# Seven up-projection channel tiles of a decoder layer computed by seven block products

## The chip, the cores and the metric

The kernel runs on one core of one Trainium2 chip. The metric is the device time of one execution in microseconds. Time before: 835.13 us, the median of 3 runs (834.89 to 835.53).

## The reference

One decoder layer for 512 tokens of width 1024, in float32. What matters here is its end, the channel mixer:

```python
u2 = _rmsnorm(h, norm2_g[l])
z = _causal_dwconv(u2 @ w_ffn_up[l], ffn_dw_w[l], ffn_dw_b[l])
h = h + (jax.nn.silu(z[..., :FFN_DIM]) * z[..., FFN_DIM:]) @ w_ffn_down[l]
return _rmsnorm(h, final_g)
```

FFN_DIM is 2816, so the up projection has 2 x 22 tiles of 128 channels: tile i is the gate (the half that goes through silu), tile 22 + i the value. The depthwise convolution is causal and three wide. Before this part stand the input projection, a convolution branch, a gated linear attention branch and the projection w_o, whose result is added to the residual.

## The kernel before

**Precision.** A float32 product is made of three: every operand is split into a high part (a cast to fp32r) and a low part (the rest), and `mm3` (L328) multiplies low by high, high by low and high by high into one PSUM bank. TensorE has the two parts of one operand as its stationary tile (128 x 128) and streams the other.

**Weights.** `order` (L162 to L178) lists every weight block in the order of use. `load` (L184) takes the next of the list into one of four `raw` buffers with a transfer issued by SyncE, four blocks ahead. `split_weight` (L254) makes the parts: ScalarE casts raw to `whi` (L281), VectorE subtracts to `wlo` (L290). For blocks in the set `ADDED` (L44) the low part is made otherwise: ScalarE writes the negated high part (L283), and a transfer in GpSimd's queue adds the same weights from DRAM (L284 is its issue). `whi` and `wlo` have four buffers each. `weight` (L299) hands a block out and splits up to `LOOK` = 2 further ones; it also calls `fill` (L312), which issues pieces of side work from `chains`, so many for each block.

**The up projection.** A channel tile is made by `col_tile` (L336): 8 k tiles (the 1024 inputs, 128 at a time) times three products, 24 products with the weights as stationary tile and all 512 tokens streaming. `GROUPS` (L34) lists 11 pairs of channel tiles, in three groups of 4, 3 and 4. For each pair (p, q) of a group: gate and value tile of p, `first_of_pair` (L1257), then gate and value tile of q, `second_of_pair` (L1265). Both call `glu` (L1243): per tile one ScalarE operation and two VectorE operations read the PSUM bank (`ffn_conv`, L1235), then a silu on ScalarE and a product on VectorE. They then form the sums and differences of halves of the two results that the down projection needs, and split them. The very first pair of group 0 is made in two halves of 256 tokens (L1358 to L1362), since the second half of the tokens is ready later.

**Seven block products.** The projections w_r, w_o and w_down are computed already by a scheme that cuts both operands in 2 x 2 blocks and needs seven block products instead of eight, with sums of blocks as operands. `seven` (L1128) runs it for w_o and, after each group, for w_down; its steps are named a11, a12, s1, n2, s4, n3 and a22, in the order of `STEPS` (L48). The sums of weight blocks are made by accumulating transfers in GpSimd's queue (`sum_on` L243, `add_n3` L232) and on VectorE (L240).

**PSUM.** Five banks have the tag `mm`, three `ax` (L124 to L128). A new tile of a tag waits until a bank of that tag is released by its readers.

**Between w_o and the up projection.** `o_complete` (L1212) makes the normed rows of a token tile as soon as its residual is complete. `to_channels` (L424) turns them with eight transposes into two `ax` banks, and `spread_gain` (L413) multiplies by the gain and splits: per bank four ScalarE operations of 128 x 128 for the high parts (L420) and four VectorE operations for the low parts (L422). Token tiles 0 and 1 are turned within w_o's last steps (`o_at`, L1219), tiles 2 and 3 between the first up tiles (L1361).

The order of the instructions on each engine is fixed when the program is built: they are queued by priority in the order written, and one that isn't ready lets later ones go ahead.

Of the kernel before, what the change touches and what calls it, by code (L numbers as in the profile page):

```python
# [17 lines left out]
P = 128  # L18
# [25 lines left out]
ADDED = {("w_glu", 2 * k) for k in range(1, KT)} | {(name, m) for name in ("w_gb", "w_gla") for m in range(KT)}  # L44
SEVEN = {"w_o": KT // 2, "w_down": FT // 2, "w_r": KT // 2}
# [27 lines left out]
def trunk_layer(ctx: ExitStack, tc: tile.TileContext, a: dict, out: bass.AP):  # L73
# [102 lines left out]
    for gi, pairs in enumerate(GROUPS):  # L176
        order += [("w_up", j) for pair in pairs for i in pair for j in (i, FT + i)]
        order += [("w_down", (pairs, step, d)) for step, d in STEPS]  # L178
# [5 lines left out]
    def load():  # L184
        if len(raws) < len(order):
            name, j = order[len(raws)]
            if name in SEVEN:
                raws.append(load_block(name, *j))
                return
            raw = raw_tile()  # L190
            nc.sync.dma_start(raw, a[name][j])
            raws.append(raw)
# [49 lines left out]

    def sum_on(name, pairs, step, d):  # L243

        where = {"a11": (0, 1), "n2": (1, 0)}
        if name == "w_r":
            where["s1"] = (1, 1)
            if (step, d) in (("n2", 1), ("s4", 0)):
                add_n3(name, pairs, 0 if step == "n2" else 1)
        if step in where:  # L250
            nxt = block(name, pairs, d, *where[step])
            nc.gpsimd.dma_start(kept[pairs, d], nxt, accum_op=ALU.add)  # L252

    def split_weight(between=None):  # L254
        if len(ready) < len(order):
# [4 lines left out]
            if name in SEVEN:  # L260
                raw = operand(name, raw, *spec)
                n = raw.shape[-1]
                hi = wp.tile([P, D], F32R, tag="whi", name=nm("whi"), bufs=4)[:, :n]
# [3 lines left out]
                sum_on(name, *spec)  # L267
# [145 lines left out]
    def spread_gain(banks, which, dst, groups=(0, 1)):  # L413
        for g in groups:
            c = which * KT + g * 4
            parts = [
                (*dst(g, k), banks[g][:, k * P : (k + 1) * P], gains[:, c + k : c + k + 1]) for k in range(4)
            ]
            for hi, _, tr, gain in parts:
                nc.scalar.activation(hi, tr, AF.Copy, scale=gain)  # L420
            for hi, lo, tr, gain in parts:
                nc.vector.scalar_tensor_tensor(lo, tr, gain, hi.bitcast(F32), ALU.mult, ALU.subtract)  # L422

    def to_channels(x, u, t, which):  # L424
        part = lambda g, k: tuple(u[g][i][:, k, t * P : (t + 1) * P] for i in range(2))
        spread_gain(turned(x), which, part)
# [792 lines left out]
    def o_at(step, i):  # L1219
        if (step, i) == ("n3", 1):  # L1220
            u2.extend(new_acts())
            to_channels(normed[0], u2, 0, 1)
        if (step, i) == ("a22", 0):
            to_channels(normed[1], u2, 1, 1)
# [8 lines left out]
    gain3 = load_gain("final_g")  # L1233
# [23 lines left out]
    def first_of_pair(i, accs):  # L1257

        w = fp.tile([P, 3 * H], F32, tag="w", name=nm("w"), bufs=2)
# [5 lines left out]
    def second_of_pair(i, accs, w, acts):  # L1265

        f = fp.tile([P, T], F32, tag="f", name=nm("f"), bufs=2)
        glu(i, accs, f)
        v = fp.tile([P, 3 * H], F32, tag="v", name=nm("v"), bufs=2)
# [80 lines left out]

    for gi, pairs in enumerate(GROUPS):
        acts = []
        early = {}
        if gi == 0:
# [3 lines left out]
            for lo in (0, T // 2):  # L1358
                for j, (w, acc) in enumerate(zip(ws, accs)):
                    col_tile(w, acts2, acc, lo, lo + T // 2)  # L1360
                    if lo == 0 and 1 <= j <= 2:  # L1361
                        to_channels(normed[j + 1], u2, j + 1, 1)  # L1362
            early = {pairs[0][0]: accs[:2], pairs[0][1]: accs[2:]}

# [3 lines left out]
        for p, q in pairs:  # L1368
            w, found = first_of_pair(p, both(p))
            acts.append(second_of_pair(q, both(q), w, found))  # L1370
        if gi < len(GROUPS) - 1:
# [93 lines left out]
```

## Time and profile before

| | |
|---|---|
| median of 3 runs | 835.13 us |
| profiled execution | 836.23 us |
| span of its instructions | 834.2 us |
| granted TensorE clock | 0.999 |
| feed-forward part (first up product to last full-width down product) | 479.3 to 824.5 us |
| VectorE busy in it | 253.99 us |
| ScalarE busy in it | 163.14 us |

Times in the profile are microseconds from the start of the span. PE is TensorE's matmul, PEld its weight load, DVE VectorE, ACT ScalarE, POOL GpSimd, SP SyncE; L281 is line 281 of the kernel. A group is written as line, engine, operation, out<-in, shapes, then x and the number of instructions, the busy time in us, the mean duration in ns, and the idle time of the engine before them with what ended it. A row of waits reads: engine, tile and line that waited, whom for, us in total, times, longest. A row of a timeline reads: start, duration, engine, line, operation, out<-in, shapes, number. A row of stages reads: stretch, its length, then for PE, PEld, DVE, ACT and POOL the busy time and the number of instructions, the granted clock, the share of the DMA engines and GB/s. A row of transfers gives the number, KB each and the median us from issue to landing.

### The profile page before, as it was taken

To read this page: it belongs to the slowest core of one execution; us is meant where nothing else is said; L and a number is where in the kernel's file an instruction comes from. 1 tells how busy PE (TensorE), PEld (TensorE's weight loads), DVE (VectorE), ACT (ScalarE), POOL (GpSimd) and SP (SyncE) were. 2 spreads that over 40 slices of the span, in tenths; PEclk is the share of its full clock that TensorE was granted. 3 is DMA by queue.
4 is the path that set the end of the run, shared out by engine and by line. 5 is a ranking of instruction groups with operands and counts; after the bars stand their busy time and mean duration, and the time that the engine had idled before them with its cause. 6 is when DMAs were issued, how large, how long until landed. Compare 5 with 4: busy or idle time off the path is not lost.

```text
span 834.2 us, 10185 instructions
## 1 busy us (share of the span) xinstructions
PE 823.8 (99%) x3817; PEld 686.7 (82%) x3817; DVE 645.3 (77%) x957; ACT 415.9 (50%) x606; POOL 69.6 (8%) x95
## 2 busy tenths in 40 slices
PE   9999999999999999999999999999999999999996
PEld 7888887888888888888888798888888888888885
DVE  5999966989899991865789658778757787667696
ACT  6853437762533553148534765444434444444454
POOL 1000102000111121000001000001000010000111
PEclk9999999999999999999999999999999999999999
DMA  9875547732546578321447544234842348222462
GB/s 341 273 214 140 137 125 158 221 101 86 128 113 157 131 199 197 102 84 57 138 100 188 169 150 140 89 97 104 214 152 88 66 87 286 98 88 97 101 126 102
DMA packets 41377, 117.72 MB, mean 141 GB/s; under 512 B 3984, under 2 KB 12448, under 8 KB 41328
## 3 DMA queue, kind: packets, MB, share of 16 engines
q1 hardware_dynamic: 33232, 88.82, 31.3%
q0 software_dynamic: 7920, 28.05, 20.0%
q8 instruction: 30, 0.49, 0.2%
q10 hardware_dynamic: 176, 0.20, 0.1%
q14 instruction: 19, 0.16, 0.1%
HBM read 114.96 MB, written 6.29 MB: 145 GB/s over the span
## 4 chain that ended last, share of the span: by engine, by line
PE 86%; DMA 4%; issue 4%; ACT 2%; DVE 2%; POOL 1%; SPq 0%; POOLq 0%; ACTq 0%; DVEq 0%
PE mm L332 26%; PE mm L333 26%; PE mm L334 26%; DMA kept<-in_w_o_dram 2%; PE mm L581 1%; PE ax L332 1%; PE ax L999 1%; PE ax L333 1%; PE ax L334 1%; DMA x<-in_x_dram 1%; DMA kept<-rows 1%; DMA raw<-in_w_o_dram 1%; PE ax L1001 1%; PE ax L981 1%; DMA hres<-in_x_dram 1%
## 5 line engine op out<-in xcount | busy, mean ns | idle before, releaser
L332 PE MATMUL mm<-uh,wlo 128*128 128x512 f32 (+1 forms) x704 | 269.8, 383 | 0.0
L334 PE MATMUL mm<-uh,whi 128*128 128x512 f32 (+1 forms) x704 | 267.3, 380 | 0.0
L333 PE MATMUL mm<-ul,whi 128*128 128x512 f32 (+1 forms) x704 | 267.1, 379 | 0.0
L688 DVE SCALAR_TENSOR_TENSOR c<-h,pp,c 128x507 f32<-128x507 f32 (+21 forms) x240 | 162.3, 732 | 1.2 <-ACT c L685 0.6
L333 PEld LDWEIGHTS mm<-ul,whi 128*128 128x128 f32 x704 | 132.5, 188 | 25.0 <-ACT h L1082 0.2
L332 PEld LDWEIGHTS mm<-uh,wlo 128*128 128x128 f32 x704 | 132.5, 188 | 24.9 <-issue 0.2
L334 PEld LDWEIGHTS mm<-uh,whi 128*128 128x128 f32 x704 | 132.4, 188 | 25.0
L281 ACT CAST whi<-raw 128x1024 fp32r<-128x1024 f32 x108 | 112.0, 1044 | 55.7 <-PE mm L334 45.6
L1240 DVE SCALAR_TENSOR_TENSOR tmp<-mm,pp,tmp 128x511 f32<-128x511 f32 x88 | 65.9, 748 | 66.7 <-ACT tmp L1238 65.5
L290 DVE TENSOR_TENSOR wlo<-raw,whi 128x1024 fp32r<-128x1024 f32 x85 | 103.2, 1220 | 14.7 <-ACT whi L281 14.4
L1238 ACT ACTIVATE tmp<-mm,pp 128x512 f32<-128x512 f32 x44 | 34.3, 779 | 60.8 <-PE mm L334 60.8
L283 ACT ACTIVATE wlo<-raw 128x1024 fp32r<-128x1024 f32 x23 | 24.4, 1061 | 74.0 <-PE mm L332 68.5
L266 DVE TENSOR_TENSOR wlo<-kept,whi 128x1024 fp32r<-128x1024 f32 (+1 forms) x40 | 46.4, 1167 | 15.4 <-ACT whi L265 15.2
L265 ACT CAST whi<-kept 128x1024 fp32r<-128x1024 f32 (+1 forms) x40 | 40.1, 1006 | 33.5 <-PE mm L334 14.3
L265 ACT CAST whi<-raw 128x1024 fp32r<-128x1024 f32 (+1 forms) x30 | 29.8, 1005 | 20.1 <-PE mm L334 18.8
L266 DVE TENSOR_TENSOR wlo<-raw,whi 128x1024 fp32r<-128x1024 f32 (+1 forms) x30 | 34.6, 1166 | 5.3 <-ACT whi L265 5.2
L1160 DVE TENSOR_TENSOR hres<-hres,mm 128x512 f32<-128x512 f32 (+1 forms) x49 | 32.6, 671 | 3.4 <-PE mm L334 2.8
L252 POOL DMA_DIRECT2D kept<-in_w_down_dram x12 | 10.3, 859 | 271.8 <-DVE wlo L266 271.8
L333 PE MATMUL mm<-wlo,sh 128*128 128x512 f32 x66 | 25.8, 391 | 0.0
L334 PE MATMUL mm<-whi,sh 128*128 128x512 f32 x66 | 25.7, 389 | 0.0
L332 PE MATMUL mm<-whi,sl 128*128 128x512 f32 x66 | 25.5, 389 | 0.0
L333 PE MATMUL mm<-h,whi 128*128 128x512 f32 x64 | 25.0, 391 | 0.0
(293 smaller groups left out, 1307.6 us busy)
## 6 DMA issues: line engine op xcount, KB each, us to landing
raw<-in_w_up_dram SPq DMA_DIRECT2D x44, 512.0 KB, 3.5
raw<-in_w_glu_dram SPq DMA_DIRECT2D x16, 512.0 KB, 6.5
raw<-in_w_down_dram SPq DMA_DIRECT2D x15, 512.0 KB, 3.3
kept<-in_w_down_dram POOLq DMA_DIRECT2D x10, 512.0 KB, 5.5
raw<-in_w_v_dram SPq DMA_DIRECT2D x8, 512.0 KB, 5.9
rows<-in_w_r_dram SPq DMA_DIRECT2D x16, 256.0 KB, 6.3
raw<-in_w_qk_dram SPq DMA_DIRECT2D x8, 512.0 KB, 3.4
raw<-in_w_gb_dram SPq DMA_DIRECT2D x8, 512.0 KB, 3.6
```

Source lines behind the costliest of these rows:

```text
L265: nc.scalar.copy(hi, raw)
L266: pace[0] = nc.vector.tensor_tensor(lo, raw, hi.bitcast(F32), ALU.subtract)
L281: nc.scalar.copy(hi, raw)
L283: nc.scalar.activation(lo, raw, AF.Copy, scale=-1.0)
L290: pace[0] = nc.vector.tensor_tensor(lo, raw, hi.bitcast(F32), ALU.subtract)
L332: nc.tensor.matmul(acc, ll, rh, start=first, stop=False, **kw)
L333: nc.tensor.matmul(acc, lh, rl, start=False, stop=False, **kw)
L334: nc.tensor.matmul(acc, lh, rh, start=False, stop=last, **kw)
L688: nc.vector.scalar_tensor_tensor(y[:, s:], c[:, : T - s], w, y[:, s:], ALU.mult, ALU.add)
L1160: nc.vector.tensor_tensor(hres[t, n][:, c], hres[t, n][:, c], x[:, c], op)
L1238: nc.scalar.activation(z, acc, AF.Identity, bias=pp[:, PP_FB + m : PP_FB + m + 1], scale=w[2])
L1240: nc.vector.scalar_tensor_tensor(z[:, s:], acc[:, : T - s], w[j], z[:, s:], ALU.mult, ALU.add)
```

## The change

Seven q tiles (6, 7, 10, 11, 14, 15, 18) get their gate and value tile by seven block products. The blocks are: the gate and the value tile of q, by two halves of the k tiles, by two halves of 256 tokens. Each step is four k tiles times three products of 256 columns. The accumulators are two `ax` banks and two `mm` banks; where a partial result belongs in two places ScalarE copies it (once negated), and later products go on adding in the bank that the copy was written to. Between the steps the eight k tiles of the partner's value tile (FT + p) are multiplied as plain products, one or two at a time (`beside`), and `first_of_pair` for p comes after step s4.

Each such tile takes four entries of the list in place of two: b (gate weights), x (the sum of blocks, from the value weights), n and m. VectorE makes two sums and GpSimd two; the second raw block, the sum and m's parts use raw buffers too.

The sums of activations are formed once, as a chain of 16 pieces of side work before the first such tile. `to_channels` now multiplies a whole bank by the gain on VectorE, keeps the result in float32 (`fu`), and casts and splits it in one operation each. Token tile 0 is turned after the first half of step n3, not the second.

The 18 tiles of nine plain channel tiles (1, 3, 4, 5, 9, 20, 13, 16, 17) join `ADDED`. The tiles w and v have one buffer each, not two, f is one of the `tmp` tiles, and the final gain is loaded before the last w_down.

```diff
+UP_SEVEN = (6, 7, 10, 11, 14, 15, 18)
+UP_BESIDE = (1, 3, 4, 5, 9, 20, 13, 16, 17)
+ADDED |= {("w_up", j) for i in UP_BESIDE for j in (i, FT + i)}
...
+            order += [("w_up7", (i, s)) for s in "bxnm"] if i in UP_SEVEN else [("w_up", i), ("w_up", FT + i)]
...
+    def up_operand(raw, i, s):
...
+        if s == "x":
+            both = kept[i, "sum"] = raw_tile()
+            add(nc.vector, both[:, :T], r0[:, :T], r1[:, :T])
+            add(nc.vector, both[:, T:], both[:, :T], r1[:, T:])
+            add(nc.gpsimd, r1[:, :T], r1[:, :T], r1[:, T:])
+            add(nc.gpsimd, r0[:, T:], r0[:, T:], both[:, T:])
+        return {"b": r0, "x": kept.get((i, "sum")), "m": r0[:, T:], "n": r1}[s]
...
+                if name == "w_up7" and spec[1] == "m":
+                    both = wp.tile([P, D], F32R, tag="raw", name=nm("wm"), bufs=4)
+                    nc.scalar.copy(both[:, :T], raw)
+                    nc.vector.tensor_tensor(both[:, T:], raw, both[:, :T].bitcast(F32), ALU.subtract)
...
+            f = fu[t, g] = dst(g)
+            nc.vector.tensor_tensor(by_token(f), by_token(bank[g]), gain, ALU.mult)
+            hi, lo = (u[g][i][:, :, t * P : (t + 1) * P] for i in range(2))
+            nc.scalar.copy(hi, by_token(f))
+            nc.vector.tensor_tensor(lo, by_token(f), hi.bitcast(F32), ALU.subtract)
...
+    def up_seven(i, beside, done):
+
+        n0, n1, bx, by = mm_bank(), mm_bank(), ax_bank(), ax_bank()
+        x, y = bx[:, :H], by[:, :H]
+
+        def step(name, acc, w, c, opens, more):
+            for k in range(4):
+                s = slice(c * T + k * P, c * T + (k + 1) * P)
+                mm3(acc, (w[0][:, s], w[1][:, s]), moving(name, k), opens and k == 0, k == 3, not opens)
+            for _ in range(more):
+                beside()
+
+        wb, wx, wn, wm = (weight("w_up7", (i, s), 0) for s in "bxnm")
+        step("a11", x, wb, 0, True, 1)
+        nc.scalar.copy(n0[:, :H], x)
+        step("s1", y, wx, 0, True, 1)
+        ys = att.rearrange("p a c -> p (a c)")[:, :H]
+        nc.scalar.copy(ys, y)
+        step("n2", x, wx, 1, False, 1)
+        prefetch(1)
+        nc.scalar.activation(n1[:, :H], x, AF.Copy, scale=-1.0)
+        step("a12", n0[:, :H], wb, 1, False, 2)
+        prefetch(2)
+        step("n3", x, wn, 0, False, 1)
+        nc.scalar.copy(n0[:, H:], x)
+        step("s4", n1[:, :H], wn, 1, False, 2)
+        nc.vector.tensor_tensor(n1[:, H:], ys, x, ALU.subtract)
+        nc.vector.tensor_tensor(n1[:, :H], ys, n1[:, :H], ALU.add)
+        done()
+        prefetch(3)
+        step("a22", n0[:, H:], wm, 0, False, 0)
+        prefetch(4)
+        return n0, n1
...
         for p, q in pairs:
+            if q in UP_SEVEN:
+                gate = col_tile(weight("w_up", p), acts2)
+                products = by_parts(weight("w_up", FT + p))
+                value, first = [], []
+                beside = lambda: value.append(next(products))
+                accs = up_seven(q, beside, lambda: first.append(first_of_pair(p, [gate, value[0]])))
+                acts.append(second_of_pair(q, accs, *first[0]))
+                continue
```

Of the new functions not shown, `by_parts` makes the plain tile three products at a time, `moving` picks the part of the activations or of their sums that a step streams, and `up_sums` is the chain of side work (forms of 128 x 512 on VectorE, then cast and low part).

123 lines of the change are left out of this document (96 added, 27 removed).

## The prediction, made before the changed kernel ran

> **What bounds the kernel now.** First the head of the page: who is busy, and at which clock.
>
> ```profile
> span 834.2 us, 10185 instructions
> ...
> PE 823.8 (99%) x3817; PEld 686.7 (82%) x3817; DVE 645.3 (77%) x957; ACT 415.9 (50%) x606; POOL 69.6 (8%) x95
> ...
> PEclk9999999999999999999999999999999999999999
> ```
>
> TensorE is busy 99% at full clock; VectorE has 23% of the span free, ScalarE half. A busy PE may still be waiting, so next come the lists of who PE and its weight load waited for, here the longest row after the start in each.
>
> ```profile
> PE ax L411 <- DVE ul L422: 1.2, 1, 1.2
> ```
>
> ```profile
> PEld ax L411 <- ACT un L431: 0.7, 2, 0.5
> ```
>
> Both belong to the transposes between w_o and the up projection. No product of the feed-forward part is in the first list. The stages, with the number of instructions after each busy time:
>
> ```profile
> 601.00:623.00 22.00, 22.00 (x99) 18.23 (x98) 12.16 (x14) 8.28 (x9) 0.00 (x0) 1.00 0.43 134
> 623.00:645.00 22.00, 22.00 (x99) 18.23 (x98) 15.71 (x22) 10.11 (x13) 0.00 (x0) 1.00 0.30 96
> ...
> 753.00:775.00 22.00, 22.00 (x99) 18.23 (x98) 15.71 (x22) 10.35 (x14) 0.00 (x0) 1.00 0.30 96
> ...
> sum 345.20, PE 344.93 PEld 289.36 DVE 253.99 ACT 163.14 POOL 19.45; mean PE 21.56 PEld 18.08 DVE 15.87 ACT 10.20 POOL 1.22
> ```
>
> From 479.3 to 824.5 PE is busy 344.93 of 345.20 us: only fewer or shorter products shorten this part, and every wait put in lengthens it. A pair's stretch of 22 us holds 15.7 us of VectorE and 10.3 of ScalarE. What a product costs is its pitch, start to start, since durations overlap:
>
> ```profile
> 461.62 0.39 PE L334 MATMUL mm<-whi,sums 128*128 128x512 f32 x1
> ...
> 470.46 0.39 PE L334 MATMUL mm<-whi,sums 128*128 128x512 f32 x1
> ```
>
> ```profile
> 490.29 0.36 PE L332 MATMUL mm<-uh,wlo 128*128 128x256 f32 x1
> 490.49 0.28 PE L333 MATMUL mm<-ul,whi 128*128 128x256 f32 x1
> ...
> 493.96 0.28 PE L332 MATMUL mm<-uh,wlo 128*128 128x256 f32 x1
> ```
>
> 39 steps of 512 columns take 8.84 us, 226.7 ns each; 29 steps of 256 columns take 3.47 us, 119.7 ns each. Half the width costs 53% of the pitch.
>
> **The change, part by part.** The sum is made against the profiled execution, 836.23 us (span 834.2, 2.03 around it); the median of the timed runs is 1.10 lower.
>
> *The products.* A pair of channel tiles by plain products is 48 products of 512 columns, 48 x 0.2267 = 10.88 us. Seven blocks of four k tiles and three products are 84 of 256 columns, 84 x 0.1197 = 10.05 us. That saves 0.83 us a tile, **5.8 us** for seven: an eighth of the columns goes (1.36 us a tile), and 0.53 of it is lost to the pitch of narrow products. The Trainium skill, "TensorE: Matmul & The Clock Gate", section "Back-to-back issue gap", gives columns over 2.4 GHz plus 2.5 ns, which would make 0.2158 and 0.1092 us and a saving of 1.19 us a tile, 8.3 in all. This trace agrees with its slope (107.0 ns per 256 columns) and not with its fixed part (12.7 ns here), and the sum goes by the trace.
>
> *From w_o to the up projection.* Rows of before:
>
> ```profile
> 465.18 1.34 ACT L431 ACTIVATE un<-hres,rstd 128x512 f32<-128x512 f32 x2
> ```
>
> ```profile
> 470.69 1.03 PE L411 MATMUL ax<-ident,un 128*128 128x128 f32 x8
> ...
> 474.31 0.60 PE L411 MATMUL ax<-ident,un 128*128 128x128 f32 x4
> 476.10 0.63 PE L411 MATMUL ax<-ident,un 128*128 128x128 f32 x4 [1.19 <-DVE ul L422]
> ```
>
> The transposes of token tile 0 move ahead by the twelve products of n3's second half (12 x 0.2267 = 2.72 us), to 467.97; their input is done at 466.52, so PE finds it. The two ax banks that they fill are now freed by one VectorE multiplication each (0.68 us, L548 below) where four ScalarE casts and four VectorE operations had to pass, and so the 1.19 us wait of tile 1's second four goes. Next late would be tile 1's own parts: multiplication, cast and low part twice, in the 2.72 us of a22's second half; ScalarE's 18 small casts of 0.39 become eight of 0.62. I take a gain of **1.4 us** (1.2, and 0.2 of the 0.7 at tiles 2 and 3); ends 1.9 (both waits gone) and a loss of 1 (VectorE's 1.22 us splits get ahead of tile 1's parts).
>
> *Work added beside PE.*
>
> ```profile
> L290 DVE TENSOR_TENSOR wlo<-raw,whi 128x1024 fp32r<-128x1024 f32 x85 | 103.2, 1220 | 14.7 <-ACT whi L281 14.4
> ...
> L1240 DVE SCALAR_TENSOR_TENSOR tmp<-mm,pp,tmp 128x511 f32<-128x511 f32 x44 | 33.0, 749 | 65.5 <-ACT tmp L1238 65.5
> ...
> L1254 DVE TENSOR_TENSOR yl<-w,yh 128x512 fp32r<-128x512 f32 x11 | 7.6, 692 | 6.9 <-ACT yh L1253 6.9
> ...
> L548 DVE TENSOR_TENSOR f<-ax,gains 128x512 f32<-128x512 f32 x4 | 2.6, 684 | 0.0
> ...
> L1160 DVE TENSOR_TENSOR hres<-hres,mm 128x256 f32<-128x256 f32 x2 | 0.8, 420 | 0.0
> ```
>
> ```profile
> L281 ACT CAST whi<-raw 128x1024 fp32r<-128x1024 f32 x108 | 112.0, 1044 | 55.7 <-PE mm L334 45.6 <-issue 10.1
> ...
> L1238 ACT ACTIVATE tmp<-mm,pp 128x512 f32<-128x512 f32 x44 | 34.3, 779 | 60.8 <-PE mm L334 60.8
> ...
> L283 ACT ACTIVATE wlo<-raw 128x1024 fp32r<-128x1024 f32 x23 | 24.4, 1061 | 74.0 <-PE mm L332 68.5
> ...
> L1253 ACT CAST yh<-w 128x512 fp32r<-128x512 f32 x11 | 6.8, 621 | 29.1 <-DVE w L1261 29.1
> ...
> L1100 ACT CAST h<-h 128x256 fp32r<-128x256 f32 x4 | 1.6, 406 | 5.0 <-DVE h L1092 5.0
> ```
>
> VectorE per seven tile: two sums of 512 (1.37), low parts of three wide blocks and a half one (3 x 1.22 + 0.69), two bank operations (0.84): 6.56 in place of 2 x 1.22, so +4.1. Each transferred low part takes 1.22 off it and adds 1.06 to ScalarE. The chain of activation sums before the first seven tile costs VectorE some 11.6 (8 x 0.69 forms, 8 low parts), ScalarE 8 x 0.62. Over the feed-forward part: 254 + 7 x 4.1 - 18 x 1.22 + 11.6 is 272 of about 339 us, 80%. A seven pair with a transferred partner needs 15.7 + 4.1 - 2.4 = 17.4 of VectorE in 20.9 us; pairs (8,10) and (12,14), whose partners stay with VectorE, 19.8. ScalarE: 10.3 + 1.04 + 0.62 + 4 x 0.41 + 2.1 = 15.7. All of it fits beside PE, and costs nothing by amount; PE covers it, not by much in the two latter pairs.
>
> *The new waits.* Between a bank's last product and the next one into it lie, by the interleaved plain products (0.68 a k tile), 2.8 us or more of PE work (k tile, step of 1.44, k tile); a ScalarE copy of 0.41 behind a cast and a negation (1.04 + 1.06) is done in 2.5: nothing. After a22 of one seven tile PE has 6.9 us (a plain tile of 5.44 and a step) before it wants a bank that may still hold the tile's result; VectorE has ahead of that result's two 0.75 reads the partner's convolution (1.5), its product and parts (1.8), a split (1.22) and two sums (1.37), some 7.4 us less what it did before a22 ended. I charge 0.3 us at each of four such successions, 1.2; ends 0 and 1.5 each. At the end of group 0 the seven tile (7) is last: PE wants the partner's a11 low part 2.04 us on (9 products), but its value tile ends 1.44 before a22 does, and cast 0.78, two reads 1.5, product 0.69, difference 0.42, cast 0.62 and low part 0.69 end 3.3 to 3.6 us on: late by 1.5, of which other products of the step can cover a part; 1.0, ends 0 and 4. For the sums of the first seven tile 0.3, ends 0 and 2. **2.5 us** in all. Single w and v buffers, f among the tmp tiles and the later load of the final gain cost nothing: their readers are done a plain tile (5.44 us) or more before the next writer, and the gain is wanted after several w_down steps of 5.4.
>
> *The transferred low parts* add POOL issues and 9.4 MB; the DMA engines stand at 0.30 in such stretches.
>
> ```profile
> L284 POOL DMA_DIRECT2D wlo<-in_w_gb_dram x8 | 7.0, 878 | 107.4 <-ACT wlo L283 107.4
> ...
> L1309 POOL TENSOR_TENSOR var<-ss,var 128x1 f32<-128x1 f32 x4 | 1.2, 292 | 18.8 <-ACT junk L1294 18.8
> ...
> L159 POOL MEMSET att<- 128x512 f32 x1 | 0.5, 524 | 0.0
> ...
> L149 POOL MEMSET shares<- 128x128 f32 x1 | 0.2, 205 | 0.0
> ```
>
> ```profile
> wlo<-in_w_gb_dram POOLq DMA_DIRECT2D x8, 512.0 KB, 6.1
> ...
> wlo<-in_w_glu_dram POOLq DMA_DIRECT2D x7, 512.0 KB, 7.2
> ```
>
> Behind a seven tile the next plain tile gets its buffer only when step n2 has ended; PE then has 4 steps and 6 k tiles, 9.8 us, before it wants the low part. Negation 1.06 and 6.1 to 7.2 to landing leave 1.5 to 2.6 us: nothing.
>
> Sum: 836.23 - 5.8 - 1.4 + 2.5 = 831.5, at the median's level **830.4 us**.
>
> **The rivals.**
> - *Low parts land late* (other side). Six tiles (5, 9, 20, 13, 16, 17) follow a seven tile. ScalarE works in order; if the negation comes up more than 1.5 to 2.6 us after n2's end, PE waits. At 4 us it is about 2 us each: 830.4 + 12 = 842.4. For: ScalarE is 75% full in these pairs, and POOL has two new adds in its queue. Against: the same transfers run behind w_gb and w_gla and the wait lists show no product waiting for one.
> - *VectorE becomes the bound.* POOL's two new adds per seven tile have no row; from a 128x1 add (0.29) and three streams at the memsets' slope (319 ns for 384 elements) they lie between 0.3 and 1.5 us, and I take 1.0. If each held VectorE up, (8,10) and (12,14) would need 21.8 us in 20.9, the four successions cost their 1.5 and group 0's end its 2.0 or more: 830.4 + 4.8 + 1.0 = 836.2, ends 833.5 and 839. The Trainium skill, "SBUF — State Buffer", section "Who interferes with whom", has such a rule: a VectorE instruction with two SBUF inputs and a GpSimd one that reads SBUF exclude one another. No run here shows it yet.
> - *The narrow products don't keep their pitch* (the change doesn't do what it says). The first 256-column product after transposes took 0.20 to the next, 0.08 more. If every change between steps and plain products cost that, 15 a tile, it is 8.4 us: 838.8. Against: within the stream the accumulator banks change at no cost.
> - *No wait at all*: 836.23 - 5.8 - 1.9 - 1.1 = 827.4.
> - *Narrow products at half the wide pitch*, 0.1133: 9.5 us saved instead of 5.8, 826.7. The page named first leans this way; the 119.7 ns above speak against it.
>
> **How the numbers follow.** Forecast 0.57 (828.5 to 833.4); no wait 0.08; half pitch 0.03; VectorE 0.16; low parts late 0.10; pitch lost 0.06. About 0.2% (1.7 us) is what a measurement of this kernel can tell from no change, so the first three are faster (0.68); of VectorE's case 0.12 is the same and 0.04 slower, and with the two others slower is 0.20. The range, 827 to 838, leaves out the half pitch, the late parts and most of the lost pitch.
>
> **What would show it.** The page should show about 84 x 7 = 588 more 256-column products and 336 fewer of 512, PE's pitches unchanged, no 1.2 wait at L411, and PE waits of a few us in all between 479 and the end, the longest near the first w_down step. Wrong if PE waits for wlo of a plain tile after a seven one, if mm products wait for VectorE reads of mm by more than 1 us a tile, or if VectorE's operations beside POOL's adds are longer than 0.7 (512) and 1.22 (1024).

## The result, and the profile after

The changed kernel took **833.68 us**, the median of 16 runs (832.08 to 835.15), where the kernel before took 835.41 (16 runs, 834.32 to 837.33): a ratio of **0.9975, 95% interval 0.9967 to 0.9984**, so 1.7 us less (1.3 to 2.8). Forecast were 4.7 us less, 830.4. The sign is right, the time lies in the range, and the size is little more than a third.

First the head of the page of the changed kernel.

```profile
span 832.5 us, 10904 instructions
...
PE 820.5 (99%) x4069; PEld 692.7 (83%) x4069; DVE 666.2 (80%) x985; ACT 451.6 (54%) x650; POOL 106.3 (13%) x127
...
PEclk9999999999999999999999999999999999999999
```

The 252 products more are 588 narrow ones more and 336 wide ones fewer, as the change says. Next, the stretch from the first up product to the start of the last 512-column product, as a row of stages of before and then of after.

```profile
479.33:824.37 345.04, 344.77 (x1618) 289.23 (x1617) 253.83 (x353) 163.11 (x223) 19.45 (x24) 1.00 0.44 123
```

```profile
479.59:822.48 342.89, 341.29 (x1871) 295.62 (x1870) 273.36 (x384) 200.28 (x278) 55.99 (x56) 1.00 0.57 151
```

The part is 2.15 us shorter. PE was idle 0.27 us in it and is now idle 1.60; VectorE has 273 us of work (the forecast said 272), ScalarE 200 in place of 163, and the DMA engines' share rose from 0.44 to 0.57. Whom PE waited for in that stretch of after:

```profile
PE mm L364 <- DVE ul L454: 0.6, 2, 0.4
PE ax L363 <- ACT mm L1462: 0.5, 1, 0.5
PE ax L363 <- ACT mm L1456: 0.3, 1, 0.3
PE mm L363 <- ACT whi L295: 0.2, 1, 0.2
```

L454 makes the low parts of the turned activations, for the first pair of tiles. L1462 and L1456 are the ScalarE copies of partial results, which the forecast charged nothing. No product waits for a transferred low part.

Cut at the first product of each stage, the part looks like this in several kernels (us, differences of product starts in the timelines; the middle ones are the experiments below):

```
                  before  after | turning  transfers  no group 0  no 7   adds on   no         neither
                                  alone    no sevens   sevens            VectorE   transfers  (e13)
early pair         25.43  25.90 |  25.18    25.64       26.53     25.93   25.92     25.27      25.15
rest of group 0    65.31  65.09 |  65.31    65.31       65.31     64.56   63.79     64.15      63.77
w_down 0           38.08  38.84 |  38.08    38.08       38.08     38.08   38.98     39.06      39.13
group 1            65.28  63.98 |  65.28    65.28       63.97     63.97   63.98     63.78      63.79
w_down 1           28.77  28.77 |  28.77    28.77       28.77     28.79   28.77     28.82      28.77
group 2            87.04  85.17 |  87.04    87.04       85.16     85.16   85.24     84.80      84.80
w_down 2           35.13  35.14 |  35.13    35.13       35.13     35.14   35.14     35.14      35.13
sum               345.04 342.89 | 344.79   345.25      342.95    341.63  341.82    341.02     340.54
```

Groups 1 and 2, with five of the tiles, give 1.30 + 1.87 = 3.17 us of the 4.15 that 0.83 a tile would be. Group 0, with the two others, gives 0.22 of 1.66, and the w_down behind it and the early pair take 0.76 + 0.47 back. A second profile of each kernel has the same stages to 0.3 us, most to 0.02, while the start of w_o's products moved by 2.6 us from run to run, with nothing changed ahead of it; so single terms are read from stages and not from whole times.

### The profile page after: what moved, and what is told of

Read it like the earlier page. It is cut to its first block, busy times and chain, and to the rows that moved or that the text cites. A ratio compares the mean times of both kernels' runs of the same rounds, so it can differ in the third digit from the quotient of the medians.

```text
span 832.5 us, 10904 instructions
## 1 busy us (share of the span) xinstructions
PE 820.5 (99%) x4069; PEld 692.7 (83%) x4069; DVE 666.2 (80%) x985; ACT 451.6 (54%) x650; POOL 106.3 (13%) x127
## 4 chain that ended last, share of the span: by engine, by line
PE 66%; DVE 17%; DMA 7%; issue 4%; ACT 3%; POOL 2%; SPq 0%; POOLq 0%; ACTq 0%; DVEq 0%
PE mm L364 20%; PE mm L363 20%; PE mm L365 20%; DVE c L716 7%; DVE wlo L296 2%; PE ax L363 2%; PE ax L364 2%; PE ax L365 2%; DMA raw<-in_w_down_dram 2%; POOL rstd L411 1%; DMA kept<-rows 1%; DMA h<-in_x_dram 1%; PE mm L609 1%; DMA hres<-in_x_dram 1%; DVE hres L1188 1%
## 5 line engine op out<-in xcount | busy, mean ns | idle before, releaser
L363 PE MATMUL mm<-uh,wlo 128*128 128x512 f32 (+1 forms) x620 | 234.5, 378 | 0.0
L364 PE MATMUL mm<-ul,whi 128*128 128x512 f32 (+1 forms) x620 | 232.1, 374 | 0.6 <-DVE ul L454 0.6
L365 PE MATMUL mm<-uh,whi 128*128 128x512 f32 (+1 forms) x620 | 231.6, 374 | 0.0
L365 PEld LDWEIGHTS mm<-uh,whi 128*128 128x128 f32 x620 | 116.7, 188 | 21.1
L364 PEld LDWEIGHTS mm<-ul,whi 128*128 128x128 f32 x620 | 116.9, 189 | 20.0 <-DVE ul L454 1.1
L314 ACT ACTIVATE wlo<-raw 128x1024 fp32r<-128x1024 f32 x41 | 43.5, 1060 | 75.9 <-PE mm L363 68.7
L295 ACT CAST whi<-raw 128x1024 fp32r<-128x1024 f32 (+1 forms) x51 | 51.7, 1024 | 44.7 <-PE mm L365 31.9
L321 DVE TENSOR_TENSOR wlo<-raw,whi 128x1024 fp32r<-128x1024 f32 x53 | 64.3, 1221 | 11.0 <-ACT whi L312 10.2
L296 DVE TENSOR_TENSOR wlo<-raw,whi 128x1024 fp32r<-128x1024 f32 (+1 forms) x51 | 62.9, 1243 | 9.2 <-ACT whi L295 8.6
L315 POOL DMA_DIRECT2D wlo<-in_w_up_dram x18 | 15.6, 864 | 98.0 <-ACT wlo L314 87.5
```

The costliest lines, as they stand in the source:

```text
L295: nc.scalar.copy(hi, raw)
L296: pace[0] = nc.vector.tensor_tensor(lo, raw, hi.bitcast(F32), ALU.subtract)
L314: nc.scalar.activation(lo, raw, AF.Copy, scale=-1.0)
L321: pace[0] = nc.vector.tensor_tensor(lo, raw, hi.bitcast(F32), ALU.subtract)
L363: nc.tensor.matmul(acc, ll, rh, start=first, stop=False, **kw)
L364: nc.tensor.matmul(acc, lh, rl, start=False, stop=False, **kw)
```

## The experiments

The line of thought up to the first runs: the products do what was forecast, group 0 loses them again through late bank copies and a late last pair, and the turning between w_o and the up projection gave nothing since its wait was one execution's chance. The rivals: the change itself makes w_o's products wait, the narrow products lose time among the wide ones, or VectorE with its new work sets the time. Each run had the kernel before on the same chip beside it.

### Each kernel again

> The kernel before, unchanged, for a second profile of it. Theory A (part of the shortfall, the wait of some 1.2 us in w_o near 449 us that the changed kernel's profile shows and the one of before does not, is the chance arrival of the eight residual row blocks and no effect of the change): the wait of VectorE for hres is between 0.3 and 4 us here and differs from execution to execution. Theory B (the change brings that wait): it stays at 0.3 us and PE has no gap over 0.3 us between 440 and 460 us. The feed-forward part, first up product to last full-width down product, takes 345.3 us within 0.3 by both.

> The changed kernel, unchanged, for a second profile and more timings. Both theories: ratio to before 0.997 to 0.9985; feed-forward part 343.1 us within 0.4, 2.2 under before; PE's waits on the two ScalarE bank copies in the second seven tile of group 0 recur, 0.4 to 0.7 us each with the restart of the pipeline. A: the wait in w_o is anything from 0 to 1.5 us. B: it is 1.0 to 1.5 us again.

Before again: 835.07 us (one run). After again: 832.99 (8 runs), ratio 0.9972 (0.9962 to 0.9982). From w_o's first product to the first up product, as rows of stages, of before, of before again, of after, and of the run with the new turning alone (below):

```profile
438.05:479.33 41.28, 40.09 (x186) 33.17 (x184) 32.65 (x50) 25.52 (x49) 4.63 (x6) 1.00 0.66 179
```

```profile
437.71:478.08 40.37, 40.34 (x185) 33.10 (x184) 32.35 (x50) 25.39 (x49) 4.57 (x6) 1.00 0.66 183
```

```profile
438.30:479.59 41.29, 40.24 (x186) 33.11 (x184) 33.87 (x46) 23.66 (x37) 4.56 (x6) 1.00 0.67 184
```

```profile
438.41:478.31 39.90, 39.90 (x185) 33.19 (x184) 34.19 (x46) 23.85 (x37) 4.63 (x6) 1.00 0.68 188
```

PE idles 1.19 us in the first row, 0.03 in the second. The 1.19 us wait from which the forecast took its 1.4 is the difference, and before again hasn't got it. Its list of waits over the whole span, of which the rows at the transposes' line L411 are these, has nothing of the low parts (L422):

```profile
PE ax L411 <- DMA x<-in_x_dram: 0.5, 1, 0.5
...
PE ax L411 <- ACT un L431: 0.3, 1, 0.3
```

Where the wait came from stands in ScalarE's timeline ahead of the transposes, of before and then of before again:

```profile
467.65 1.05 ACT L265 CAST whi<-kept 128x1024 fp32r<-128x1024 f32 x1 [1.13 <-DMA kept<-in_w_o_dram]
```

```profile
466.43 1.04 ACT L265 CAST whi<-kept 128x1024 fp32r<-128x1024 f32 x1
```

In the first execution the cast of w_o's last weight sum waited 1.13 us for the transfer that adds to it, and everything behind it came late; in the second it did not wait.

The third row has 1.05 us of idling of another kind, a product of w_o itself that waits for VectorE's low part:

```profile
PE ax L364 <- DVE wlo L296: 1.1, 1, 1.1
```

VectorE stood there 3.9 us behind a load of residual rows. In after again this gap is absent (39.90 in all), and in the runs below it comes and goes (39.90 to 41.50). So this too is the arrival of a transfer in one execution and no effect of the change.

### The new turning and the transfers without any seven tile

```diff
-UP_SEVEN = (6, 7, 10, 11, 14, 15, 18)
+UP_SEVEN = ()
...
-            chains.append(up_sums())
```

> No tile by seven block products and no chain of activation sums; the new turning between w_o and the up projection and the 18 transferred low parts stay. A: only the 1.4 us of the turning are gained, 834.0 us, ratio 0.9983 (0.9975 to 0.999), the products of the feed-forward part at 345.3 us, VectorE 22 us less busy than before in it, ScalarE 19 more less 2 for the casts. Rival C (the transfers alone cost time, by late low parts or by DMA): slower than before, ratio over 1.000, and PE waits for wlo of up tiles.

834.52 us (11 runs), ratio 0.9988 (0.9979 to 0.9997). All stages behind the early pair are those of before; the early pair is 0.21 longer. The gain in groups 1 and 2 is the seven products' alone. The other small parts of the change (single w and v buffers, f among the tmp tiles, the later load of the final gain) stay in this run and in the next, so they cost nothing behind the early pair.

### The turning alone

```diff
-UP_SEVEN = (6, 7, 10, 11, 14, 15, 18)
-UP_BESIDE = (1, 3, 4, 5, 9, 20, 13, 16, 17)
+UP_SEVEN = ()
+UP_BESIDE = ()
...
-            chains.append(up_sums())
```

> Only the new turning at the transposes: no seven tiles, no activation sums, no transferred low parts (those 18 weight tiles are split by VectorE as before). Theory A (the 1.19 us wait of the profile of before was one execution's chance, so the new turning is worth little): from the start of w_o's products to the first up product 39.9 us, where it was 41.28 and 40.37 in the two profiles of before; 0.2 to 0.5 given back in the early pair; ratio 0.9985 to 1.0000. Rival (the prediction's term is right): 1.4 us faster, ratio 0.9983, with the early pair at 25.4. For the transfers beside it: if they do nothing of their own, all stages behind the early pair are as in before and in the run without seven tiles, to 0.05 us.

835.54 us (11 runs), ratio 0.9997 (0.9988 to 1.0006): 0.25 us, with an interval from 1.0 gained to 0.5 lost. From w_o to the up projection its trace is 1.38 us shorter than the first profile of before, which looks like the forecast's 1.4, and 0.47 shorter than the second; the early pair is 0.25 shorter, not longer. That the early pair is 25.64 us in the run above and 25.18 here is not the work of the transfers, although they are the only difference in the kernel: the run above writes its first negated high part at 494.4 us, and its extra time lies in a wait at 478 us, behind a w_o cast that waited 0.38 us for the same transfer as in the profile of before.

### Group 0 without seven tiles

```diff
-UP_SEVEN = (6, 7, 10, 11, 14, 15, 18)
+UP_SEVEN = (10, 11, 14, 15, 18)
```

> Seven block products for 10, 11, 14, 15 and 18 alone; group 0 plain, all else as in the changed kernel. A: group 0's two tiles save 1.66 us of products and give back more (waits on bank copies 1.1, first pairs 0.5, its w_down 0.8), so without them the kernel is 0.3 to 1 us faster than the changed one, ratio to before 0.9963 to 0.9972 if the changed one is at 0.9975. Rival D (every seven tile gives its 0.6 to 0.8 wherever it stands): 1.2 to 1.7 us slower than the changed one, ratio 0.999 to 0.9995.

832.01 us (5 runs), ratio 0.9962 (0.9950 to 0.9975). From the first up product to the last it is as long as after (342.95 against 342.89), with five seven tiles in place of seven. Group 0 is back at 65.31 and the first w_down at 38.08, so group 0's two tiles gain 0.22 and lose 0.76. The early pair came out at 26.53, 0.6 longer than in after. Its trace shows why: the cast that waited in the first profile of before waited here too, and these rows of PE's waits stand at the start of the up projection.

```profile
467.70 1.05 ACT L295 CAST whi<-kept 128x1024 fp32r<-128x1024 f32 x1 [1.17 <-DMA kept<-in_w_o_dram]
```

```profile
PE mm L364 <- DVE ul L454: 1.2, 2, 0.8
...
PE mm L363 <- ACT uh L453: 0.4, 1, 0.4
```

PE waits 0.41 and 0.76 us for the parts of token tile 1, where it waits once, 0.16 us, in the run with the new turning alone. So with the transfer 1.17 us late the new turning loses about 1 us as well, at the first up products and no longer at the transposes. (The other 0.40 of the first row is the wait that after has at 494 us.)

### Group 0 without its last seven tile

```diff
-UP_SEVEN = (6, 7, 10, 11, 14, 15, 18)
+UP_SEVEN = (6, 10, 11, 14, 15, 18)
```

> Seven block products for all but tile 7, so that group 0 ends with a plain pair. A: its w_down takes 38.1 us again, not 38.8 (the operands of the last pair are in time), and the two waits on bank copies, which belong to the second seven tile of the group, go; group 0's up part after the first pair 64.5 to 64.7 us (one tile saving 0.7) instead of 65.1 to 65.4. In all 1.2 us under the changed kernel, ratio 0.9957 to 0.9965. Rival (the chain of activation sums in VectorE's queue is what holds group 0 up, with one seven tile as with two): w_down 38.1, but the up part still 65.1 to 65.4.

833.06 us (5 runs), ratio 0.9969 (0.9957 to 0.9981). Group 0 takes 64.56, 0.75 less than before for one tile, and the first w_down 38.08: one tile less by seven products, and the sum is 1.26 us shorter than in after. Tile 7 as the last of the group cost more than it saved.

### A bank copy ahead of the weight casts

```diff
-        prefetch(1)
         nc.scalar.activation(n1[:, :H], x, AF.Copy, scale=-1.0)
+        prefetch(1)
```

> The negated bank copy is written ahead of the split of the next plain tile, so ScalarE takes it first. Theory A (the seven tiles lose what the products save because the bank copies wait in ScalarE's order behind casts and behind an operation that itself waits for VectorE): in groups 1 and 2 the second and third seven tile take 21.0 us from tile to tile like the first, not 21.2; groups 1 and 2 (up parts) together 148.6 instead of 149.15 us, group 0's wait on the negated copy goes; 0.6 to 1.2 us faster than the changed kernel, ratio to before 0.996 to 0.9968. Rival (the narrow products themselves lose it where their operands or banks change): stages as in the changed kernel, within 0.1 us.

**838.8 us** (10 runs), ratio 1.0038 (1.0026 to 1.0049): slower than before, by moving one ScalarE copy of 0.36 us ahead. The waits of PE from the first up product on:

```profile
PE ax L363 <- DVE wlo L296: 1.7, 3, 0.9
PE mm L363 <- DMA wlo<-in_w_up_dram: 1.3, 2, 1.0
PE ax L363 <- ACT mm L1456: 0.6, 1, 0.6
```

The second row is the forecast's rival "low parts land late", at plain tiles behind a seven tile. The first is the step before: raw blocks that come late, so that VectorE's sum, then ScalarE's cast, then VectorE's low part are late, here at 750 us:

```profile
749.82 0.69 DVE L257 TENSOR_TENSOR raw<-raw,raw 128x512 f32<-128x512 f32 x1 [1.64 <-DMA raw<-in_w_up_dram]
...
752.52 1.05 ACT L295 CAST whi<-raw 128x1024 fp32r<-128x1024 f32 x1 [3.81 <-DVE raw L257]
```

Group 1 took 65.05 us, 1.1 more than in after, and group 2 88.29, 3.1 more.

### The same move without group 0's seven tiles

```diff
-UP_SEVEN = (6, 7, 10, 11, 14, 15, 18)
+UP_SEVEN = (10, 11, 14, 15, 18)
...
-        prefetch(1)
         nc.scalar.activation(n1[:, :H], x, AF.Copy, scale=-1.0)
+        prefetch(1)
```

> Both: seven block products for 10, 11, 14, 15 and 18 alone, and the negated copy first. A: 0.5 us under the same without the copy moved (832.0 us in its runs, ratio 0.9962): ratio 0.9955 to 0.996, groups 1 and 2 at 63.8 and 84.8 us. Rival: as without the move, 63.97 and 85.16 us.

833.24 us (7 runs), ratio 0.9968 (0.9957 to 0.9979). Group 1 took 64.18 (64.0 without the move), group 2 84.90 (85.16), the w_down between them 29.07 (28.77): the move gains and loses 0.3. The large loss of group 2 is not there, and why group 0's tiles decide on it is not settled.

### The same move without transfers

```diff
-UP_BESIDE = (1, 3, 4, 5, 9, 20, 13, 16, 17)
+UP_BESIDE = ()
...
-        prefetch(1)
         nc.scalar.activation(n1[:, :H], x, AF.Copy, scale=-1.0)
+        prefetch(1)
```

> The negated copy of a seven tile's bank moved ahead of the weight casts, as in the run that came out slower than before, but without the 18 transferred low parts. Theory A (that run lost its time because the low parts by transfer landed late: one more or earlier ScalarE operation shifts the negations and the chain of raw buffers): no such loss here, group 1 63.5 to 63.9, group 2 84.4 to 84.9, no wait of PE for wlo by DMA (there is none), ratio 0.9935 to 0.9955. Rival (the copy's order itself delays the casts and so VectorE's low parts): group 2 87 us or more, w_down 0 39 or more, ratio above 0.998.

831.07 us (5 runs), ratio 0.9949 (0.9935 to 0.9962); groups 1 and 2 at 63.79 and 84.80, the same as without transfers and without the move. So the loss in groups 1 and 2 needs the transfers: without them the copy's order delays no cast that PE notices.

### GpSimd's additions on VectorE

```diff
-            add(nc.gpsimd, r1[:, :T], r1[:, :T], r1[:, T:])
-            add(nc.gpsimd, r0[:, T:], r0[:, T:], both[:, T:])
+            add(nc.vector, r1[:, :T], r1[:, :T], r1[:, T:])
+            add(nc.vector, r0[:, T:], r0[:, T:], both[:, T:])
```

> The two sums of weight blocks that GpSimd makes per seven tile are made by VectorE. If a VectorE operation with two operands in SBUF and a GpSimd one exclude each other (the changed kernel's trace has a 512 sum of VectorE at 1.73 us and a low part at 1.88 us, both beside a GpSimd add of 1.29 us), none of VectorE's operations of these shapes is longer than 0.75 and 1.25 us here, and 14 x 1.4 us more of its own work stand against it: feed-forward part within 0.5 us of the changed kernel's 342.9 to 343.1. Rival (VectorE is full and its amount of work decides): 1 to 3 us slower, most in pairs 8 and 12.

833.59 us (5 runs), ratio 0.9967 (0.9955 to 0.9979). Group 0 falls from 65.09 to 63.79, which is its two tiles' full 1.66 to 0.14; the sum by 1.07. In after, the late copy at tile 7 stands behind an operation that waited for VectorE, and the last negation of a weight block had ended 15 us before:

```profile
556.03 0.63 ACT L1274 ACTIVATE tmp<-tmp 128x512 f32<-128x512 f32 x1 [1.96 <-DVE tmp L1268]
...
558.03 0.36 ACT L1456 COPY mm<-ax 128x256 f32<-128x256 f32 x1
```

What held VectorE up, and what this run takes away, is seen a little earlier:

```profile
547.60 1.29 POOL L257 TENSOR_TENSOR raw<-raw 128x512 f32<-128x512 f32 x1 [3.28 <-DVE raw L257]
547.71 1.73 DVE L257 TENSOR_TENSOR raw<-raw,raw 128x512 f32<-128x512 f32 x1
...
550.99 1.29 POOL L257 TENSOR_TENSOR raw<-raw,raw 128x512 f32<-128x512 f32 x1 [2.10 <-DVE wlo L296]
551.49 1.88 DVE L296 TENSOR_TENSOR wlo<-raw,whi 128x1024 fp32r<-128x1024 f32 x1
```

and in the groups of VectorE, of after and then of this run (line, operation, shapes, number | busy us, mean ns | idle before):

```profile
L296 DVE TENSOR_TENSOR wlo<-raw,whi 128x1024 fp32r<-128x1024 f32 x36 | 46.4, 1297 | 7.2 <-ACT whi L295 6.7
...
L257 DVE TENSOR_TENSOR raw<-raw,raw 128x512 f32<-128x512 f32 x14 | 13.9, 990 | 4.9 <-ACT whi L295 4.9
```

```profile
L296 DVE TENSOR_TENSOR wlo<-raw,whi 128x1024 fp32r<-128x1024 f32 x36 | 43.6, 1218 | 6.6 <-ACT whi L295 6.2
...
L257 DVE TENSOR_TENSOR raw<-raw,raw 128x512 f32<-128x512 f32 x21 | 14.4, 684 | 5.6 <-DMA raw<-in_w_up_dram 5.5
L257 DVE TENSOR_TENSOR raw<-raw 128x512 f32<-128x512 f32 x7 | 4.8, 682 | 0.0
```

Beside a GpSimd addition that starts before it, a VectorE operation with two SBUF inputs ends about when that one has ended and its own time has passed: 1.73 us for 0.68, 1.88 for 1.22. With fourteen more additions VectorE is busy 2.5 us more in these two kinds (62.8 for 60.3), since those that it had already became as short as they are alone. The Trainium skill, "SBUF — State Buffer", section "Who interferes with whom", says that a VectorE instruction with two SBUF inputs contends with a GpSimd instruction that reads SBUF, and calls the shared pair of ports an exclusive lock; these rows agree.

### The same without tile 7

```diff
-UP_SEVEN = (6, 7, 10, 11, 14, 15, 18)
+UP_SEVEN = (6, 10, 11, 14, 15, 18)
...
-            add(nc.gpsimd, r1[:, :T], r1[:, :T], r1[:, T:])
-            add(nc.gpsimd, r0[:, T:], r0[:, T:], both[:, T:])
+            add(nc.vector, r1[:, :T], r1[:, :T], r1[:, T:])
+            add(nc.vector, r0[:, T:], r0[:, T:], both[:, T:])
```

> The version that the runs so far point to: both sums that GpSimd made for a seven tile are VectorE's, and up tile 7 goes back to plain products, tile 6 and the five of the other groups stay with seven. Theory A (two separate losses in group 0: GpSimd's adds hold VectorE up, and a seven tile as the group's last makes its last pair late for w_down): the first w_down stage 38.1 us as before, the rest of group 0 64.5 (before 65.31, less 0.83 for one tile), groups 1 and 2 64.0 and 85.2, up start to the last 512 product 341.2 to 341.6, and a ratio to the kernel before of 0.995 to 0.9965. Rival (without the second seven tile of the group the adds hold nothing up, so moving them brings nothing here): group 0 64.56 and 341.63 as in the run without tile 7 alone, the same to 0.1. Rival (the adds on VectorE are too much for it): a stage of 0.5 us or more longer than in the run without 7.

832.52 us (6 runs), ratio 0.9963 (0.9950 to 0.9976), 341.56 us of up projection and w_down against 341.63 without 7 alone. The first rival holds: where no second seven tile follows at once, the held-up VectorE has time to catch up and moving the additions brings nothing.

### No transfers

```diff
-UP_BESIDE = (1, 3, 4, 5, 9, 20, 13, 16, 17)
+UP_BESIDE = ()
```

> All seven seven-tiles, but none of the 18 low parts by transfer: VectorE splits those weight tiles. Theory A (VectorE is near its bound in a pair with a seven tile, so the transfers buy the room): such a pair needs 15.7 + 4.1 us of VectorE, and some 1.2 more where GpSimd's adds hold it up, 21.0 in the 20.9 that PE takes; with the last tiles of a group standing next to each other, group 1 and 2 grow by 0.5 to 3 us together over 63.98 and 85.17, group 0 by 0.5 to 2 over 65.1, VectorE named in PE's waits; 834 to 838, ratio 0.999 to 1.003. Rival (the load of VectorE decides nothing, the transfers are idle): all stages as in the kernel after to 0.1 us, ratio 0.997.

**831.76 us** (5 runs), ratio 0.9950 (0.9937 to 0.9964). Neither theory had this: the transfers are not idle, and they don't buy room; they cost. The row of the stretch:

```profile
480.23:821.25 341.02, 340.46 (x1871) 295.73 (x1869) 293.25 (x403) 185.97 (x261) 42.43 (x38) 1.00 0.43 124
```

VectorE has 20 us more to do than in after (293 of 341, 86%), ScalarE 14 less, PE idles 0.56 in place of 1.60, and the part is 1.87 us shorter. Every stage that the transfers touch is shorter: early pair 0.63, group 0 and its w_down 0.72, group 1 0.20, group 2 0.37. The loss does not come from one place. In the early pair the order of VectorE's work differs, here in after, with the product that waits, and then in this run:

```profile
490.11 1.42 DVE L1410 TENSOR_TENSOR f<-f,f 128x512 f32<-128x512 f32 x2
491.45 1.28 DVE L451 TENSOR_TENSOR f<-ax,gains 128x512 f32<-128x512 f32 x2
...
493.99 0.39 PE L364 MATMUL mm<-ul,whi 128*128 128x256 f32 x1 [0.42 <-DVE ul L454]
```

```profile
490.88 1.29 DVE L451 TENSOR_TENSOR f<-ax,gains 128x512 f32<-128x512 f32 x2
```

With the transfers, the first two sums of activations (L1410) stand ahead of the gain multiplication of the last token tile (L451), and PE waits 0.42 us for its low part. All eight traces with seven tiles and transfers have this order and this wait of 0.4 us; none of the four without transfers has. In groups 1 and 2 it is ScalarE, by the waits of the weight load, of after and then of this run:

```profile
PEld ax L363 <- ACT mm L1462: 1.9, 4, 0.9
```

```profile
PEld ax L363 <- ACT mm L1462: 0.2, 1, 0.2
```

L1462 is the negated bank copy ahead of step n3. In ScalarE's timeline at such a copy, first after, then this run at the same tile:

```profile
734.32 1.06 ACT L314 ACTIVATE wlo<-raw 128x1024 fp32r<-128x1024 f32 x1
735.28 1.03 ACT L312 CAST whi<-raw 128x1024 fp32r<-128x1024 f32 x1
736.22 0.83 ACT L1281 CAST sh<-v 128x768 fp32r<-128x768 f32 x1
736.96 0.61 ACT L288 CAST wm<-raw 128x512 fp32r<-128x512 f32 x1
737.48 0.36 ACT L1462 ACTIVATE mm<-ax 128x256 f32<-128x256 f32 x1
```

```profile
733.70 1.05 ACT L312 CAST whi<-raw 128x1024 fp32r<-128x1024 f32 x1
735.42 0.84 ACT L1281 CAST sh<-v 128x768 fp32r<-128x768 f32 x1 [0.67 <-DVE v L1301]
736.17 0.36 ACT L1462 ACTIVATE mm<-ax 128x256 f32<-128x256 f32 x1
```

With transfers four operations stand back to back ahead of the copy, the negation (L314) the first; without them ScalarE even waits 0.67 us between its operations, and the copy is there 1.3 us earlier while the stage began 0.9 us earlier. Three such copies make the next product 0.17 us late each, 0.5 of the 0.57 that groups 1 and 2 lose. The transfers' traffic is a rival: the median landing of an up-projection weight block is 4.9 us in after and 3.4 here. But in groups 1 and 2 of after no wait of TensorE, VectorE or ScalarE names a transfer.

### No transfers and no tile 7

```diff
-UP_SEVEN = (6, 7, 10, 11, 14, 15, 18)
-UP_BESIDE = (1, 3, 4, 5, 9, 20, 13, 16, 17)
+UP_SEVEN = (6, 10, 11, 14, 15, 18)
+UP_BESIDE = ()
```

> No transferred low parts and up tile 7 by plain products. Theory A (the two losses are separate and add up): early pair 25.3 us, rest of group 0 64.5 or a little less, first w_down stage 38.1, group 1 63.8, group 2 84.8, so up start to the last 512 product 340.3 to 340.7, where the changed kernel has 342.9 and the run without transfers 341.0; ratio to the kernel before 0.9935 to 0.995. Rival (the end of group 0 was late because of the transfers' work on ScalarE, not because of tile 7): no gain over the run without transfers, 341.0 or more.

831.80 us (5 runs), ratio 0.9953 (0.9941 to 0.9966), sum 340.74, 0.28 better than with tile 7. w_down 0 is back at 38.09, but group 0 takes 64.90 and not 64.5: PE starts 0.25 us late at the first seven tile's step s1. The two gains add up only in part.

### No transfers, and the additions on VectorE

```diff
-UP_BESIDE = (1, 3, 4, 5, 9, 20, 13, 16, 17)
+UP_BESIDE = ()
...
-            add(nc.gpsimd, r1[:, :T], r1[:, :T], r1[:, T:])
-            add(nc.gpsimd, r0[:, T:], r0[:, T:], both[:, T:])
+            add(nc.vector, r1[:, :T], r1[:, :T], r1[:, T:])
+            add(nc.vector, r0[:, T:], r0[:, T:], both[:, T:])
```

> No transferred low parts, and GpSimd's two additions per seven tile are VectorE's: the most that VectorE can be given here, 15.7 + 4.1 + 1.4 = 21.2 us in a pair with a seven tile, where PE needs 20.9 (an estimate from means). Theory A (VectorE works ahead in the stretches between, so its amount over a group decides and not over a pair): group 0 63.7 to 64.1, w_down 38.9 to 39.1, groups 1 and 2 63.8 and 84.8, as without transfers or up to 0.4 better. Rival (VectorE is the bound as soon as it has no help): groups 0 to 2 each longer than in the run without transfers by 0.3 us or more, with VectorE named in PE's waits.

831.04 us (5 runs), ratio 0.9951 (0.9939 to 0.9963). Its row:

```profile
478.45:818.99 340.54, 340.20 (x1870) 295.94 (x1869) 292.46 (x416) 185.82 (x261) 20.54 (x24) 1.00 0.43 124
```

All the work that VectorE could be given is on it, 292 us of 341, no more than with GpSimd's help (293), since nothing holds it up; PE idles 0.34 us. VectorE is not the bound, and had no need of the transfers. The four versions without transfers agree within their intervals at 0.995; the changed kernel's interval (0.9967 to 0.9984) lies above that of e11 (0.9937 to 0.9964).

## Why the prediction was wrong

- **The products, −5.8: right.** Their pitch, from rows of after in step a11 of tile 10:

```profile
614.86 0.28 PE L363 MATMUL ax<-uh,wlo 128*128 128x256 f32 x1
...
616.17 0.28 PE L365 MATMUL ax<-uh,whi 128*128 128x256 f32 x1
```

  11 steps take 1.31 us, 119.1 ns each (119.7 forecast). Without transfers groups 1 and 2 gain 1.50 and 2.24 of 1.66 and 2.49: 0.08 us a tile is lost to the changes between narrow and wide products. The rival of the lost pitch (0.08 at every change, 15 a tile) is refuted, and so is that of the half pitch.
- **The turning, −1.4: failed.** The step "and so the 1.19 us wait of tile 1's second four goes" put the wait down to the slow freeing of two banks. What the traces show is a cast held up 1.13 us by a late transfer in that one execution. Without the lateness the kernel before has no such wait; with it (1.17 us, the run without group 0's seven tiles) the new turning loses about 1 us as well, at the first up products, where tile 1's own parts come late, as the forecast feared in its next sentence. Alone the turning is worth 0.25 us (1.0 gained to 0.5 lost), 1.1 us less than forecast.
- **The transferred low parts, "nothing": failed, and this is the largest.** Without them the part is 1.87 us shorter. The step weighed one way to lose, a late landing, and that did not happen. Of the 1.87, 0.57 are lost in groups 1 and 2, and 0.5 of them at negated bank copies that ScalarE reached late with the negations in its queue: the forecast had let such a copy stand behind a cast and a negation, and at the tile shown it stood behind two more casts. 0.63 are lost in the early pair, where two sums on VectorE come ahead of the last token tile. The other 0.72, in group 0 and its w_down, go with the transfers, but there the late copies stand behind VectorE's work and not behind a negation; how the transfers lead to it is not shown. The step's "costs nothing by amount" is right of the amount; what decides is what stands ahead of an operation that PE waits for. And the relief that the transfers were to give, VectorE's 1.22 us each, was not needed.
- **The bank copies, "nothing": failed.** At group 0's second seven tile PE waited 0.3 and 0.5 us for them, and with the restart its products were 1.3 us late. Both waits are gone when GpSimd's additions are, and also when the transfers are, so they are no price of the copies but of ScalarE running late there.
- **The new waits, +2.5: near in size, in part by luck.** Without transfers the part is 4.02 us shorter, so 5.81 − 4.02 = 1.79 are lost in waits and changes of width. The end of group 0, charged 1.0, took 0.98 (w_down 0 at 39.06), and it is tile 7's doing, since without that tile the stage is back at 38.1. But the forecast charged a wait for the partner's low part, and that took 0.2 of it. The longest wait, 0.5 us with its restart, is for the cast of a weight block 20 us into the stage, and the cast ahead of that one waited for VectorE's sum of weight blocks, here in after:

```profile
588.65 1.05 ACT L295 CAST whi<-kept 128x1024 fp32r<-128x1024 f32 x1 [2.48 <-DVE kept L249]
```

  By which path tile 7 delays it is not shown. Of the four successions, charged 1.2 together, the three in groups 1 and 2 took almost none.
- **GpSimd's additions, 1.0 us each:** 1.28 at the least and 1.4 on average. The rival "VectorE becomes the bound" had the mechanism right (the two engines do hold each other up) and its price wrong: 1.3 us in group 0, where two seven tiles follow each other with little between, nothing measured elsewhere.
- **Low parts late, 842.4:** not in the changed kernel, but one ScalarE copy away: 838.8.

Put together, −5.8 + 1.79 + 1.87 = −2.1 us for the part; it comes out because the 1.79 is what was left over. With what the turning gains ahead of the part (0.47 in one trace, by the times not to be told from nothing), that agrees with the measured 1.7 (1.3 to 2.8), and with 2.3 (1.5 to 3.2) in the second comparison. Open are how the transfers make group 0 late, why group 2 lost only where group 0 had seven tiles and the copy came first, and whether the turning alone gains anything.

## What to carry to other kernels

A wait in one profile is a wait of one execution: before its removal is counted as a gain, follow it back to what was late, and look for it in a second profile of the same kernel, above all where it stands behind a transfer. Moving work from an engine that is 86% busy to one that is 55% busy (VectorE and ScalarE without the transfers) can cost time, when the second engine has short copies in its queue that the busiest engine waits for, or when the move changes the order of the work on the first: count what stands ahead of such an operation, not the engine's share. And give GpSimd no elementwise work beside a VectorE that is on a tight schedule, unless the rows show that VectorE's two-input operations keep their length.

## What the runs showed of the hardware

A VectorE operation with two SBUF inputs that starts 0.11 us after a GpSimd addition of 1.29 us takes 1.73 us, alone 0.68: it waits for nearly the whole addition. GpSimd's 128x512 addition takes 1.28 us at the least, 1.9 times VectorE's 0.68. And a 256-column product keeps its pitch of 119 ns among 512-column ones, so two widths can be interleaved at 0.08 us for some 15 changes.
